# Gate projections of the first layer: float32 products in four column groups in place of split products

## The chip, the core and the metric

The kernel runs on one core of a Trainium2 chip. The metric is the device time of one launch in microseconds (us). Everything below is about the first 30 us of a program that takes about 1465 us.

## The reference

A trunk of two decoder layers over 512 positions of width 1024. Layer 0 mixes tokens by a gated DeltaNet, layer 1 by a Conformer convolution module; each layer then attends to a memory of 256 positions and applies a squared-ReLU MLP. Every sub-layer has an RMS norm before it and a residual after it. The change touches the beginning of layer 0:

```python
h = rms_norm(x, dn_norm)                      # (x * rsqrt(mean(x*x) + eps)) * g
proj = h @ w_in                               # 1024 x (4*1024 + 16)
qkv, z = proj[..., :3072], proj[..., 3072:4096]
b_raw  = proj[..., 4096:4104]                 # one column for each of 8 heads
a_raw  = proj[..., 4104:4112]
qkv = silu(causal_depthwise_conv(qkv, w_conv))
beta = sigmoid(b_raw)
g = -exp(a_log) * softplus(a_raw + dt_bias)
# q, k, v, beta and g then go through the chunked gated delta rule
```

All of it is float32. The sixteen columns of b_raw and a_raw are the "ab" of this document: beta and the decay g of the heads come from them.

## The kernel before, in words

**Products.** Every large matrix product is made of three products in the format fp32r. A tile is split into a high part (a cast to fp32r) and a low part (the tile minus its high part, also fp32r); the kernel sums high·high, high·low and low·high. `mm3` and `proj` issue these three for each of the 8 slices k of 128 input channels (`KT` = 8). Weights arrive as raw float32 tiles of 128 x 1024; ScalarE casts the high part `wh` (L251) and VectorE subtracts to get `wl` (L71). Such a tile serves one output block of 128 channels over all k.

**The input and its norm.** `x` arrives transposed in eight tiles of 128 channels x 512 positions (`load_x`, L103, on the SP queue). `Norm.parts` makes `xh` (ScalarE, L378: x times the norm's gain g, to fp32r) and `xl` (VectorE, L77: x times g minus xh). The factor 1/rms of each position is not in them: it is found later from a second copy of x laid out by position (`xt`, squares on ScalarE at L1541, `stat_tok`), turned into a row on all partitions by TensorE (`spread`, tile `rb`), and multiplied in when a result is taken out of PSUM.

**The first pass.** Head k0 of the key projection is computed in `mm_ab` together with ab. Its weight tile comes in four pieces of 256 columns (`piece`): pieces 0 and 1 are issued on ScalarE's queue, pieces 2 and 3 on SP's between the x tiles. The gain of this norm has a small tile of its own, `gn0` (128 x 8, loaded at L117), and the 16 ab columns of the weight are `wab` (L118, 128 x 128: eight k of 16 columns). On SP's queue the order is x0, gn0, wab, x1, x2, piece 2, x3, x4, piece 3, x5, x6, x7. The order on ScalarE and VectorE is written out by hand (`pin`): a piece's split, then two x tiles' parts, and so on; after the first x tile the split of `wab` into `abp` (16 high and 16 low columns for each k).

For each k TensorE issues three products for head k0 and two for ab: abp's 32 columns (high and low) against xh, and its 16 high columns against xl. They sum into PSUM rows 0 to 31 of one bank: rows 0 to 15 hold the sum of high·high and high·low, rows 16 to 31 low·high.

**What follows.** The list `mains` gives TensorE's order: `mm_ab`, then the heads k1, k2, k3 (each through `halves`: a first part up to k = `cut` and a second part), the four q heads, z, v and so on. Between the parts `run` calls side tasks listed by position. `spread` and `gates_in` (ab times rb, on VectorE) come after the first part of head k2, which has 3 of the 8 k. `gates` comes inside its second part, after k = `CUT_G` = 5: it transposes ab (four TensorE transposes of 32 rows, tile `abT`), adds the two halves on VectorE into `abt`, and computes beta and g from it with small operations. The `ws` machinery (`wnext`, `wsplit`, `wload`) loads and splits weight tiles a few ahead.

Of the kernel before, what the change touches and what calls it, by code (L numbers as in the profile page):

```python
# [8 lines left out]
F32 = mybir.dt.float32  # L9
# [5 lines left out]
P = 128  # L15
# [22 lines left out]
def tile_trunk(ctx, tc, xT, memT, x_d, mem_d, prm_d, adt_d, bdw_d, tap_d, fin_d, w_ab, w_kq, w_v, w_z, w_dno, w_pw1, w_pw2,  # L38
# [56 lines left out]
    prm, gn0 = const([P, NPRM], "prm"), const([P, 8], "gn0")  # L95
# [18 lines left out]
    piece(act, 0)  # L114
    wab = slot(s="wab")[:, 0:P]
    def load_first():
        nc.sync.dma_start(out=gn0, in_=prm_d[:, 0:8])  # L117
        nc.sync.dma_start(out=wab, in_=w_ab)  # L118

    xin = load_x({0: load_first, 2: lambda: piece(nc.sync, 2), 4: lambda: piece(nc.sync, 3)})  # L120
# [185 lines left out]
    def halves(key, hf, xs, reg, name, cut=4, inside=None):  # L306
        st = {}

        def first():
            st["w"] = wnext(key, hf)  # L310
            reg[name] = psum("h")
            proj(st["w"], xs, reg[name], 0, cut)

        return [first, lambda: proj(st["w"], xs, reg[name], cut, 8, inside)]
# [115 lines left out]
    class DeltaNet:  # L430
# [12 lines left out]
        def gates_in(self):  # L443
            self.ab = slot(s="ab")
            tc.keep_in_program_order(tt(dve, self.ab[0:32, :], self.ps.pop("ab")[0:32, :], self.n.rb[0:32, :], ALU.mult))
            dve.tensor_copy(self.tok, self.n.tok)

        def gates(self):
            ab = self.ab
            ps_t = psum("abT")  # L450
            for c in range(4):
                pe.transpose(ps_t[:, c * 32:(c + 1) * 32], ab[0:32, c * P:(c + 1) * P], ident[0:32, 0:32])
            abt, beta, g = self.abt, self.beta, self.g
            abp = ps_t[:, 0:128].rearrange("p (c x) -> p x c", c=4)
            a3 = abt.rearrange("p (x c) -> p x c", c=4)
            dve.tensor_copy(a3, abp[:, 16:32])
            tt(dve, a3, abp[:, 0:16], a3, ALU.add)
# [1047 lines left out]
    abp = slot(F32R, "abp")[:, 0:2 * P]  # L1505
    ab3 = abp.rearrange("p (k x) -> p k x", k=KT)
# [5 lines left out]
    for i in range(4):  # L1512
        s = slice(i * 256, (i + 1) * 256)
        pin(act.copy(hl0[0][:, s], raw0[:, s]))
        pin(tt(dve, hl0[1][:, s], raw0[:, s], hl0[0][:, s].bitcast(F32), ALU.subtract))
        for k in (2 * i, 2 * i + 1):
            n0.parts(k, xin[k], pin)
            if k == 0:
                wab3 = wab.rearrange("p (k x) -> p k x", k=KT)
                pin(act.copy(ab3[:, :, 0:16], wab3))  # L1520
                pin(tt(dve, ab3[:, :, 16:32], wab3, ab3[:, :, 0:16].bitcast(F32), ALU.subtract))
# [30 lines left out]
    def mm_ab():  # L1552
        w = wnext(("k", 0), 0)
        D.ps["ab"], D.ps["k", 0] = psum("ab"), psum("h")
        for k in range(KT):
            (xh, xl), (wh, wl), ps = n0.xs[k], wk(w, k), D.ps["k", 0]
            ab = D.ps["ab"]
            pe.matmul(ps, wh, xh, start=k == 0, stop=False)
# [6 lines left out]
            pe.matmul(ab[0:16, :], abp[:, 32 * k:32 * k + 16], xl, start=False, stop=k == KT - 1)  # L1565
# [151 lines left out]
CUT_G = 5  # L1717
# [70 lines left out]
def _layout(np, i):  # L1788
# [23 lines left out]
    w = i["dn_w_in"][0]  # L1812
    r["w_ab"] = f(w[:, 4096:].reshape(8, 128, 16).transpose(1, 0, 2).reshape(128, 128))
# [32 lines left out]
```

## Time and profile before

| | |
|---|---|
| median of 3 runs | 1465.76 us (1465.67 to 1467.18) |
| profiled execution | 1465.14 us |
| its span, first to last instruction | 1463.4 us |
| TensorE busy | 1452.9 us, 99% |
| VectorE, ScalarE, GpSimd busy | 1065.2, 771.2, 266.8 us |
| first product of head k0 | at 5.36 us |
| second k of head k0 | at 8.06 us |
| first product of head k1 | at 16.35 us |

In the profile PE is TensorE's matmuls and PEld its weight loads, DVE is VectorE, ACT ScalarE, POOL GpSimd, SP the queue that issues most transfers. A row names a line of the kernel, the engine, the operation, the output and inputs with buffer numbers left out, and the shapes. Times count from the start of the span. "idle before, releaser" in a row says how long the engine had been idle and what it had waited for. Matmuls are pipelined: one starts before the duration of the one ahead has run out, so what one costs is read from the distance of their starts.

### The profile page before, as it was taken

The page shows a single profiled execution, that of the slowest core. Times are in us where ns is not written, and L with a number is a line of the kernel's source. Part 1 is how long each engine was busy: PE and PEld are TensorE (multiplying, and loading weights), DVE is VectorE, ACT ScalarE, POOL GpSimd, SP SyncE. Part 2 cuts the span into 40 slices and gives each one's busy share as a digit, 9 for nine tenths or more (in the row PEclk, how much of TensorE's full clock was granted, in tenths as well). Part 3 has the DMA queues.
Part 4 walks back from the last instruction along what each step waited for, and adds up shares of the span by engine and source line. Part 5 has one row for each costly group of instructions (what it writes and reads, how often), then busy time and mean ns, then how long its engine had stood idle before and what let it go on. Part 6 is the DMA issues. An engine that isn't in the chain of part 4 may idle for free.

```text
span 1463.4 us, 19623 instructions
## 1 busy us (share of the span) xinstructions
PE 1452.9 (99%) x7298; PEld 1225.5 (84%) x7298; DVE 1065.2 (73%) x1615; ACT 771.2 (53%) x1326; POOL 266.8 (18%) x289
## 2 busy tenths in 40 slices
PE   9999999999999999999999999999999999999997
PEld 7888889988888888888888889988888888888886
DVE  6879889867646766767679899985555776767677
ACT  7766865655434464435355655564444544434354
POOL 1411310103113000010000486402113010000100
PEclk9999999999999999999999999999999999999999
DMA  8232124442213666584766624533214566575853
GB/s 283 84 115 73 59 87 158 132 143 87 72 44 108 166 165 179 140 199 136 202 159 215 185 82 162 179 129 100 72 51 127 139 169 177 135 210 131 229 144 87
DMA packets 62735, 201.82 MB, mean 138 GB/s; under 512 B 7728, under 2 KB 10032, under 8 KB 62640
## 3 DMA queue, kind: packets, MB, share of 16 engines
q1 hardware_dynamic: 52416, 164.39, 33.4%
q0 software_dynamic: 9792, 35.66, 14.3%
q8 instruction: 57, 0.93, 0.3%
q10 hardware_dynamic: 432, 0.52, 0.1%
q14 instruction: 38, 0.31, 0.1%
HBM read 197.66 MB, written 2.10 MB: 136 GB/s over the span
## 4 chain that ended last, share of the span: by engine, by line
PE 94%; DVE 3%; ACT 2%; DMA 1%; issue 0%; POOL 0%; SPq 0%; POOLq 0%; DVEq 0%
PE up L292 8%; PE up L294 8%; PE up L293 8%; PE dn L1130 6%; PE dn L1128 6%; PE dn L1129 6%; PE pw L294 3%; PE pw L292 3%; PE pw L293 3%; PE h L292 3%; PE h L293 3%; PE h L294 3%; PE xo L293 2%; PE xo L294 2%; PE q L292 2%; PE q L293 2%
## 5 line engine op out<-in xcount | busy, mean ns | idle before, releaser
L251 ACT CAST wh<-raw 128x1024 fp32r<-128x1024 f32 x259 | 271.6, 1051 | 358.7 <-issue 97.0
L71 DVE TENSOR_TENSOR wl<-raw,wh 128x1024 fp32r<-128x1024 f32 (+1 forms) x250 | 304.2, 1219 | 104.3 <-ACT wh L251 98.5
L292 PE MATMUL up<-xh,wh 128*128 128x512 f32 x512 | 199.7, 390 | 0.0
L294 PE MATMUL up<-xh,wl 128*128 128x512 f32 x512 | 199.3, 389 | 0.0
L293 PE MATMUL up<-xl,wh 128*128 128x512 f32 x512 | 199.2, 389 | 0.0
L294 PEld LDWEIGHTS up<-xh,wl 128*128 128x128 f32 x512 | 96.1, 188 | 20.1
L293 PEld LDWEIGHTS up<-xl,wh 128*128 128x128 f32 x512 | 96.2, 188 | 19.8
L292 PEld LDWEIGHTS up<-xh,wh 128*128 128x128 f32 x512 | 96.1, 188 | 19.7
L239 POOL DMA_DIRECT2D t<-w_dn x48 | 42.1, 915 | 354.2 <-DVE wl L71 239.0
L1128 PE MATMUL dn<-wh,ah 128*128 128x512 f32 x256 | 99.8, 390 | 0.0
L1130 PE MATMUL dn<-wl,ah 128*128 128x512 f32 x256 | 99.6, 389 | 0.0
L1129 PE MATMUL dn<-wh,al 128*128 128x512 f32 x256 | 99.6, 389 | 0.0
L77 DVE SCALAR_TENSOR_TENSOR rl<-up,rb 128x512 f32<-128x512 f32 x64 | 44.1, 690 | 58.4 <-PE up L294 58.4
L1358 DVE SCALAR_TENSOR_TENSOR ca<-x,prm,ca 128x512 f32<-128x512 f32 x112 | 82.3, 752 | 3.9 <-ACT ca L1355 1.5
L251 ACT CAST wh<-t 128x1024 fp32r<-128x1024 f32 x44 | 46.4, 1055 | 55.8 <-PE dn L1129 43.7
L71 DVE TENSOR_TENSOR wl<-t,wh 128x1024 fp32r<-128x1024 f32 x44 | 53.7, 1223 | 29.5 <-ACT wh L251 29.3
L292 PE MATMUL h<-xh,wh 128*128 128x512 f32 x184 | 73.7, 400 | 0.0
L71 POOL TENSOR_TENSOR sq<-sq,sq 128x512 f32<-128x512 f32 x28 | 45.4, 1621 | 148.3 <-ACT sq L385 134.2
L294 PE MATMUL h<-xh,wl 128*128 128x512 f32 x184 | 71.9, 391 | 0.0
L293 PE MATMUL h<-xl,wh 128*128 128x512 f32 x184 | 71.7, 390 | 0.0
L71 DVE TENSOR_TENSOR acc<-acc,dn 128x512 f32<-128x512 f32 x100 | 67.3, 682 | 1.2
L71 DVE TENSOR_TENSOR al<-u,ah 128x512 fp32r<-128x512 f32 x64 | 44.1, 688 | 21.4 <-ACT ah L331 21.4
(385 smaller groups left out, 3560.1 us busy)
## 6 DMA issues: line engine op xcount, KB each, us to landing
raw<-w_dn SPq DMA_DIRECT2D x68, 512.0 KB, 3.7
raw<-w_up SPq DMA_DIRECT2D x64, 512.0 KB, 4.3
t<-w_dn POOLq DMA_DIRECT2D x48, 512.0 KB, 6.0
raw<-w_pw SPq DMA_DIRECT2D x24, 512.0 KB, 3.7
raw<-w_dn POOLq DMA_DIRECT2D x20, 512.0 KB, 5.9
raw<-w_k SPq DMA_DIRECT2D x16, 512.0 KB, 3.6
raw<-w_vv SPq DMA_DIRECT2D x16, 512.0 KB, 4.1
t<-w_dn SPq DMA_DIRECT2D x16, 512.0 KB, 3.5
```

The costliest lines, as they stand in the source:

```text
L71: r = e.tensor_tensor(out=o, in0=a, in1=b, op=op)
L77: return dve.scalar_tensor_tensor(out=o, in0=a, scalar=s, in1=b, op0=op0, op1=op1)
L239: nc.gpsimd.dma_start(out=t, in_=a, accum_op=ALU.add)
L251: ins = [act.copy(h, raw)]
L292: pe.matmul(ps, wh, xh, start=first, stop=False)
L293: pe.matmul(ps, wh, xl, start=False, stop=False)
L294: pe.matmul(ps, wl, xh, start=False, stop=last)
L1128: pe.matmul(ps, xh, w[0][:, s], start=opens and k == 0, stop=False, skip_group_check=True)
L1129: pe.matmul(ps, xl, w[0][:, s], start=False, stop=False, skip_group_check=True)
L1130: pe.matmul(ps, xh, w[1][:, s], start=False, stop=k == 3, skip_group_check=True)
L1358: first["tap"] = dve.scalar_tensor_tensor(out=a, in0=src, scalar=w, in1=a, op0=ALU.mult, op1=ALU.add)
```

## The change

The ab products are made from x itself in float32, without xh and xl. `abp` is now `wab` times the gain, a single VectorE product in float32 (16 columns for each k, and 16 zero columns behind the last). Product kk takes 32 columns of it from 16·kk on, of which the first 16 are those of slice kk, and the raw tile `xin[kk]`; it writes PSUM rows 32j to 32j + 31, j = kk mod 4. So the products kk = 0 to 3 go to four different groups of output columns of the array, and kk = 4 to 7 add to the same four. The first four are issued after k = 4 of head k0, the other four after k = 6 (`AB_AT`). The four partial sums are added after the transposes in `gates`, which are now full 128 x 128 transposes, by one VectorE reduction.

The gain `gn0` moves into the first transfer: a new input `first` has in each row 8 gain values and the 256 columns of piece 0, and is issued on ScalarE's queue in place of piece 0. `wab` moves behind x3 on the SP queue, which is then x0, x1, x2, piece 2, x3, wab, x4, piece 3, x5, x6, x7; its product with the gain is pinned behind the parts of x3.

The heads k1 and k2 issue the sixteen products with `wh` first (all k, xh and xl) and then the eight with `wl` (`HIGH_FIRST`); the first part of `halves` is now the sixteen. `CUT_G` is 7, so the transposes of `gates` stand behind the last product of head k2.

```diff
-    prm, gn0 = const([P, NPRM], "prm"), const([P, 8], "gn0")
+    prm, gn0 = const([P, NPRM], "prm"), const([P, 264], "gn0")
...
-    piece(act, 0)
+    act.dma_start(out=gn0, in_=first_d)
     wab = slot(s="wab")[:, 0:P]
-    def load_first():
-        nc.sync.dma_start(out=gn0, in_=prm_d[:, 0:8])
+
+    def load_wab():
         nc.sync.dma_start(out=wab, in_=w_ab)
 
-    xin = load_x({0: load_first, 2: lambda: piece(nc.sync, 2), 4: lambda: piece(nc.sync, 3)})
+    xin = load_x({2: lambda: piece(nc.sync, 2), 3: load_wab, 4: lambda: piece(nc.sync, 3)})
...
         def first():
             st["w"] = wnext(key, hf)
             reg[name] = psum("h")
-            proj(st["w"], xs, reg[name], 0, cut)
-
-        return [first, lambda: proj(st["w"], xs, reg[name], cut, 8, inside)]
+            if name in HIGH_FIRST:
+                for k in range(KT):
+                    for j in range(2):
+                        pe.matmul(reg[name], wk(st["w"], k)[0], xs[k][j], start=(k, j) == (0, 0), stop=False)
+            else:
+                proj(st["w"], xs, reg[name], 0, cut)
+
+        def second():
+            if name in HIGH_FIRST:
+                for k in range(KT):
+                    pe.matmul(reg[name], wk(st["w"], k)[1], xs[k][0], start=False, stop=k == KT - 1)
+                    if inside and k in inside:
+                        inside[k]()
+            else:
+                proj(st["w"], xs, reg[name], cut, 8, inside)
+
+        return [first, second]
...
-            tc.keep_in_program_order(tt(dve, self.ab[0:32, :], self.ps.pop("ab")[0:32, :], self.n.rb[0:32, :], ALU.mult))
+            tc.keep_in_program_order(tt(dve, self.ab, self.ps.pop("ab"), self.n.rb, ALU.mult))
...
-                pe.transpose(ps_t[:, c * 32:(c + 1) * 32], ab[0:32, c * P:(c + 1) * P], ident[0:32, 0:32])
+                pe.transpose(ps_t[:, c * P:(c + 1) * P], ab[:, c * P:(c + 1) * P], ident)
             abt, beta, g = self.abt, self.beta, self.g
-            abp = ps_t[:, 0:128].rearrange("p (c x) -> p x c", c=4)
-            a3 = abt.rearrange("p (x c) -> p x c", c=4)
-            dve.tensor_copy(a3, abp[:, 16:32])
-            tt(dve, a3, abp[:, 0:16], a3, ALU.add)
+            dve.tensor_reduce(out=abt.rearrange("p (x c) -> p x c", c=4),
+                              in_=ps_t.rearrange("p (c y x) -> p x c y", c=4, x=32)[:, 0:16], op=ALU.add, axis=AX.X)
...
-    abp = slot(F32R, "abp")[:, 0:2 * P]
-    ab3 = abp.rearrange("p (k x) -> p k x", k=KT)
+    abp = slot(s="abp")[:, 0:P + 16]
+    pool.memset(abp[:, P:P + 16], 0.0)
...
-        pin(act.copy(hl0[0][:, s], raw0[:, s]))
-        pin(tt(dve, hl0[1][:, s], raw0[:, s], hl0[0][:, s].bitcast(F32), ALU.subtract))
+        src = raw0[:, s] if i else gn0[:, 8:264]
+        pin(act.copy(hl0[0][:, s], src))
+        pin(tt(dve, hl0[1][:, s], src, hl0[0][:, s].bitcast(F32), ALU.subtract))
         for k in (2 * i, 2 * i + 1):
             n0.parts(k, xin[k], pin)
-            if k == 0:
-                wab3 = wab.rearrange("p (k x) -> p k x", k=KT)
-                pin(act.copy(ab3[:, :, 0:16], wab3))
-                pin(tt(dve, ab3[:, :, 16:32], wab3, ab3[:, :, 0:16].bitcast(F32), ALU.subtract))
+            if k == 3:
+                pin(tt(dve, abp[:, 0:P].rearrange("p (k x) -> p k x", k=KT), wab.rearrange("p (k x) -> p k x", k=KT),
+                       over_i(gn0[:, 0:KT], 16), ALU.mult))
...
     def mm_ab():
         w = wnext(("k", 0), 0)
         D.ps["ab"], D.ps["k", 0] = psum("ab"), psum("h")
+        ab = D.ps["ab"]
         for k in range(KT):
             (xh, xl), (wh, wl), ps = n0.xs[k], wk(w, k), D.ps["k", 0]
-            ab = D.ps["ab"]
             pe.matmul(ps, wh, xh, start=k == 0, stop=False)
             pe.matmul(ps, wl, xh, start=False, stop=False)
-            if k:
-                pe.matmul(ab[0:32, :], abp[:, 32 * k:32 * k + 32], xh, start=False, stop=False)
             pe.matmul(ps, wh, xl, start=False, stop=k == KT - 1)
-            if k == 0:
-                pe.matmul(ab[0:32, :], abp[:, 0:32], xh, start=True, stop=False)
-            pe.matmul(ab[0:16, :], abp[:, 32 * k:32 * k + 16], xl, start=False, stop=k == KT - 1)
+            if k in AB_AT:
+                for j in range(4):
+                    kk = 4 * AB_AT[k] + j
+                    pe.matmul(ab[32 * j:32 * j + 32, :], abp[:, 16 * kk:16 * kk + 32], xin[kk], start=kk == j, stop=kk > 3)
...
-CUT_G = 5
+CUT_G = 7
+AB_AT = {4: 0, 6: 1}
+HIGH_FIRST = (("k", 1), ("k", 2))
...
+    r["first"] = f(np.concatenate([r["prm"][:, 0:8], _pack_a(np, w[:, 1024:1280])[0][:, 0:256]], axis=1))
```

More of the change, by code (lines that the diff above doesn't have):

```diff
@@ L37, in tile_trunk @@
 @with_exitstack
-def tile_trunk(ctx, tc, xT, memT, x_d, mem_d, prm_d, adt_d, bdw_d, tap_d, fin_d, w_ab, w_kq, w_v, w_z, w_dno, w_pw1, w_pw2,
+def tile_trunk(ctx, tc, xT, memT, x_d, mem_d, prm_d, adt_d, bdw_d, tap_d, fin_d, first_d, w_ab, w_kq, w_v, w_z, w_dno, w_pw1, w_pw2,
                w_q, w_k, w_vv, w_o, w_up, w_dn, yT):
@@ L1812, in _layout @@
     w = i["dn_w_in"][0]
+    w = i["dn_w_in"][0]
+    r["first"] = f(np.concatenate([r["prm"][:, 0:8], _pack_a(np, w[:, 1024:1280])[0][:, 0:256]], axis=1))
     r["w_ab"] = f(w[:, 4096:].reshape(8, 128, 16).transpose(1, 0, 2).reshape(128, 128))
```

## The prediction

> **What bounds the kernel now.** First the page: busy shares, and the chain that ended last by engine.
>
> ```profile
> PE 1452.9 (99%) x7298; PEld 1225.5 (84%) x7298; DVE 1065.2 (73%) x1615; ACT 771.2 (53%) x1326; POOL 266.8 (18%) x289
> PE 94%; DVE 3%; ACT 2%; DMA 1%; issue 0%; POOL 0%; SPq 0%; POOLq 0%; DVEq 0%
> ```
>
> TensorE is busy almost throughout and the chain lies on it. Busy alone proves little, because matmul ends are modelled, so next the waits of TensorE over the whole span (us in total, times, longest).
>
> ```profile
> PE warm L130 <- POOL ones L127: 1.2, 1, 1.2
> PE h L1558 <- ACT xh L378: 1.0, 1, 1.0
> PE pw L294 <- POOL wl L71: 0.2, 1, 0.2
> PE dn L1130 <- DVE wl L71: 0.2, 1, 0.2
> ```
>
> These are all: 2.2 us at the start, 0.4 us afterwards. So the time falls by what is taken off TensorE, if its inputs keep up. The change works in the first 30 us, so third the chain in order of time (start, length, what), at the start and at some later places.
>
> ```profile
> 0.81 0.38 SPq L103
> 1.25 0.42 SPq L117
> 1.72 0.43 SPq L118
> 2.19 5.08 DMA x<-xT
> 7.29 0.73 ACT xh L378
> 8.06 0.50 PE h L1558
> ...
> 26.52 0.36 PE abT L452 x4
> 26.88 0.43 PE h L292
> ...
> 52.19 0.44 PE kt L586 x4
> 52.63 0.89 PE G L590 x8
> 53.52 0.23 PE h L292
> ```
>
> The path begins on the SP queue: x tile 1 is issued only at 2.19, behind gn (L117) and wab (L118); it lands 5.08 us later, is split, and TensorE starts k = 1 at 8.06. Fourth the timeline, which shows how closely the inputs run beside TensorE.
>
> ```profile
> 6.01 0.28 DVE L71 TENSOR_TENSOR abp<-wab,abp 128x128 fp32r<-128x128 f32 x1
> ...
> 8.04 0.75 DVE L77 SCALAR_TENSOR_TENSOR xl<-x,gn,xh 128x512 fp32r<-128x512 f32 x1 [1.75 <-ACT xh L378]
> ...
> 9.43 0.40 PE L1558 MATMUL h<-xh,wh 128*128 128x512 f32 x1
> ...
> 10.73 1.41 DVE L77 SCALAR_TENSOR_TENSOR xl<-x,gn,xh 128x512 fp32r<-128x512 f32 x2
> ...
> 12.61 0.73 ACT L378 ACTIVATE xh<-x,gn 128x512 fp32r<-128x512 f32 x1 [0.34 <-DMA x<-xT]
> ...
> 13.89 1.05 ACT L251 CAST wh<-raw 128x1024 fp32r<-128x1024 f32 x1 [0.56 <-DMA raw<-w_kq]
> ...
> 14.97 1.22 DVE L71 TENSOR_TENSOR wl<-raw,wh 128x1024 fp32r<-128x1024 f32 x1 [0.85 <-ACT wh L251]
> ...
> 16.35 0.40 PE L292 MATMUL h<-xh,wh 128*128 128x512 f32 x1
> ...
> 19.00 1.05 ACT L251 CAST wh<-raw 128x1024 fp32r<-128x1024 f32 x1
> ...
> 20.09 1.23 DVE L71 TENSOR_TENSOR wl<-raw,wh 128x1024 fp32r<-128x1024 f32 x1 [3.90 <-ACT wh L251]
> ...
> 21.82 0.39 PE L292 MATMUL h<-xh,wh 128*128 128x512 f32 x1
> ...
> 22.97 0.18 DVE L414 RECIPROCAL rstd<-sd 128x4 f32<-128x4 f32 x1 [1.66 <-ACT sd L412]
> ```
>
> A matmul's duration (0.40) is not its price, since the next one starts earlier. From 9.43 (first product of k = 2) to 16.35 (first product of head k1) there are 6 k of 5 products: 6.92 / 30 = 0.231 us each. Head k1 lasts from 16.35 to 21.82, 24 products of 0.228. The last x tile (12.61) and the second weight tile (13.89) waited for DMA, so transfers are not far behind the path.
>
> **What is removed.** Sixteen ab products at 0.231 are 3.7 us of TensorE. One cast on ScalarE and one split on VectorE go; the VectorE product of wab with gn that replaces the split has the same 128x128 shape, 0.28 (row at 6.01), now behind xl of k = 3.
>
> **What is added.** Eight float32 products of 512 columns. The nearest row is G.
>
> ```profile
> L590 PE MATMUL G<-cva 128*128 128x128 f32 x64 | 8.5, 275 | 0.0
> L1565 PE MATMUL ab<-xl,abp 128*16 128x512 f32 x8 | 3.1, 393 | 0.0
> ```
>
> The code asks for 32 G products, the trace counts 64: a float32 product is issued as two halves. In the chain eight halves took 0.89 us, 0.111 each at 128 columns; four times that, 0.445, is my estimate at 512. One after another the eight new products are 16 halves, 7.1 us, twice what is removed: the change pays only if column groups overlap. Before shows no two products at once (the ab product of 16 columns costs as much as any other, but all of them write from partition 0). So a group of four costs between two slots (the four first halves together, then the four second ones, 0.89) and eight (3.56). Going back to the h products costs 0 (after G, 0.23) to 0.20 (after abT, 0.43 instead of 0.23); I take 0.1. I take the low end, G = 0.99, because the four have different weights, different output partitions and no data between them. The Trainium skill (TensorE: Matmul & The Clock Gate, Part 3) reports a speedup of 2.38 for three column tiles; for a group here that is an estimate from that page of 3.56 / 2.38 = 1.5, by which the pass would end at 16.1 instead of the 15.1 found below. No run shown so far decides between them.
>
> **Where the pass ends.** (1) With gn and wab no longer ahead, x tile 1 is issued at 1.25, 0.94 earlier. Its landing gains between 0, if bytes are the limit, and 0.94. The windows (last columns: DMA share, GB/s) say that the DMA engines were busy but moved little while the small packets passed, so I take 0.9.
>
> ```profile
> 4.00:5.00 1.00, 1.00 (x7) 1.00 (x6) 0.29 (x1) 0.72 (x2) 0.00 (x0) 1.00 0.95 172
> ...
> 12.00:13.00 1.00, 1.00 (x6) 0.64 (x5) 1.00 (x3) 0.66 (x2) 0.00 (x0) 1.00 1.03 420
> ```
>
> (2) Then VectorE sets the pace, since TensorE needs only 0.7 us per k there. From the start of xl 1 (8.04) to the end of xl 4 (10.73 + 0.71 = 11.44) it needs 3.40. From 7.14 that gives 10.54, with the new wab product 10.82, and k = 4 is through on TensorE at 11.05. Moving wab behind x tile 3 costs nothing, as long as it lands before 9.5, when VectorE comes to it:
>
> ```profile
> 4.27 0.80 SPq L103 DMA_DIRECT2D x<-xT  x2
> ...
> wab<-w_ab SPq DMA_DIRECT2D x1, 64.0 KB, 3.2
> ```
>
> x tiles 3 and 4 were issued at 4.27 to 5.07 in before, and wab took 3.2 to land (last column), so now it lands near 8; if it came later, everything behind it on VectorE would wait, the remaining xl and so TensorE. (3) From 11.05 on TensorE has two groups and 9 products (k = 5, 6, 7): 11.05 + 9 x 0.231 + 2G = 13.13 + 2G = 15.1. The second group reads x tile 7 directly, landed by 12.61 in before and needed at about 13.5. (4) Against 16.35 that is 1.25 earlier; the break-even is G = 1.61.
>
> **What comes next.** Head k1 needs its weight cast, ready at 13.89 + 1.05 = 14.94: 0.16 of cover. So the gain cannot exceed 1.4, unless that transfer lands earlier too (0.9 at most, by the same queue). Its low part is ready at 16.19; in the old order the third product would ask for it at 15.6 and stall 0.6, in the new order (high products first) after 16 products, at 18.8. For k2 the cast is ready at 20.05, needed at 15.1 + 5.47 = 20.6; the low part at 21.32, needed at 24.2. The spread of rstd (ready 23.15) stands behind those 16 products too, 24.2, and does not wait. So the reordering of k1 and k2 costs nothing and buys 0.6. The evictions that need the spread vector come a little later with it; TensorE does not wait for them in before.
>
> **The gates.** Four 128-column transposes, as kt (0.44), in place of abT (0.36): +0.08 on the path. On VectorE one reduction takes the place of a copy and an add:
>
> ```profile
> 31.21 0.22 DVE L71 TENSOR_TENSOR abt<-abT,abt 128x64 f32<-128x64 f32 x1
> ...
> 40.19 0.37 DVE L503 TENSOR_REDUCE ind<-ident 128x4 f32<-128x128 f32 x1
> ```
>
> A copy and an add of 0.22 against one reduction of 0.37 or somewhat more, with no TensorE wait behind it in before: nothing. With the transposes behind k = 7 of head k2 they come at 26.4, as in before.
>
> **Sum.** -1.25 + 0.08 = -1.17. The profiled execution took 1465.14, 1.74 beyond its span, and lies 0.62 under the median of the runs, 1465.76; on the median that is **1464.6**.
>
> **Rivals.**
>
> *Half-chained groups.* The kernel issues both halves of product 0 before product 1. If a half that waits for its own column group holds up those behind it, only the second half of one overlaps the first half of the next: five slots per group, 2.33, the pass ends at 17.8, +1.5 in all, 1467.3. For it: every float32 row comes as pairs in program order. Against it: nothing measured. The Trainium skill (same page and part) states that matmuls start and end in program order, which is this rival; no row of before has the pattern.
>
> *No overlap, slower.* The column groups do not run at once, so the change does not do what it says: G = 3.56 + 0.1, the pass ends at 20.5, +4.2, 1470.0. For it: the ab products of before filled an eighth or a quarter of the columns and still took a full slot. It decides (over 0.2% slower) from G = 3.03 on.
>
> *A later stretch moves too.* From 142 to 188 us the chain runs on ScalarE and VectorE:
>
> ```profile
> 142.25 0.62 ACT cva L553
> ...
> 187.61 0.58 DVE z L71
> ...
> 100.00:150.00 50.00, 49.91 (x310) 41.78 (x309) 47.75 (x94) 31.84 (x66) 6.13 (x13) 1.00 0.19 64
> ```
>
> VectorE is busy 47.75 of 50 us there. If its or ScalarE's order shifts with the earlier first heads, 2 us may come on top (1462.6 or less) or be lost (up to 1468.5). Against it: the same instructions, released in the same order, all a little earlier.
>
> **Chances.** A measurement of this kernel can tell about 0.2%, 2.9 us, from no change. Forecast, with its bounds (x tile 1 not earlier at all; G up to 1.5): 0.50, all within 0.2%. Half-chained 0.20, within. No overlap 0.14, slower. Later stretch better 0.10, faster; worse 0.06, of it 0.04 slower. That makes 0.10 / 0.72 / 0.18. The range, 1462.2 to 1468.2, leaves out the serial case and the outer parts of the later stretch, 0.2 together.
>
> **What would show it.** Right: ab products of four groups starting within a few ns of each other, groups about 1 us apart from first start to next h product; first product of k = 1 near 7.1; first product of head k1 near 15.1, waiting for nothing or shortly for its cast; abT near 26.4. Wrong: groups of 2.3 or 3.6 us; x tile 1 landing at 7.2 as before; a wait for x tile 7 in front of the second group; new TensorE waits between 100 and 200 us.

## The result and the profile after

After the change the kernel took 1468.0 us, the median of 22 runs (1466.47 to 1468.9), against 1465.72 for the kernel before in 22 runs beside it: ratio 1.0013, 95% interval 1.0007 to 1.0019. It was forecast at 1464.6, that is 1.2 us faster; it is 2.3 us slower. That is within the 0.2% that the prediction takes for no change, but the interval leaves 1 out and lies on the other side. The profiled execution took 1467.88, 1.68 beyond its span of 1466.2.

The first pass did what was forecast. Rows from the timeline of TensorE after the change (start, length):

```profile
6.57 0.40 PE L1570 MATMUL h<-xh,wh 128*128 128x512 f32 x1
...
10.37 1.06 PE L1576 MATMUL ab<-x,abp 128*32 128x512 f32 x8
11.36 0.50 PE L1570 MATMUL h<-xh,wh 128*128 128x512 f32 x1
...
12.95 1.06 PE L1576 MATMUL ab<-x,abp 128*32 128x512 f32 x8
13.95 0.50 PE L1570 MATMUL h<-xh,wh 128*128 128x512 f32 x1
...
14.75 0.40 PE L315 MATMUL h<-xh,wh 128*128 128x512 f32 x1
...
26.47 0.65 PE L466 MATMUL abT<-ident,ab 128*128 128x128 f32 x4 [0.20 <-DVE ab L71]
```

A group of four with its eight halves took 0.99 and 1.00 us from its start to the next h product. Slice k = 1 started at 6.57 (before 8.06), head k1 at 14.75 (before 16.35): 1.6 us won. In the ten other profiled executions below with this first pass head k1 started at 14.82 to 15.25, and in two more with that of before at 16.33 and 16.42, so 1.1 to 1.6 us are won.

The waits of TensorE over the whole span show a new one (us in total, times, longest; the first three):

```profile
PE dt L548 <- DVE L L77: 1.7, 1, 1.7
PE warm L130 <- POOL ones L127: 1.2, 1, 1.2
PE h L294 <- DVE wl L71: 0.3, 1, 0.3
```

`dt` is the product in `decay` (L548) that needs `L`, the last result of the gates. The way there is: `grep`, the end of the gates' small operations on VectorE; `ct`, a product on TensorE that needs it; a copy on ScalarE; then gsum, R and L on VectorE. That place in the timeline of before, which the prediction did not show (rows of this chain, and one of GpSimd):

```profile
40.11 0.16 DVE L492 COPY grep<-g 128x128 f32<-128x128 f32 x1
...
41.92 0.38 PE L515 MATMUL ct<-tri_mid,grep 128*128 128x128 f32 x2
...
42.85 1.30 POOL L71 TENSOR_TENSOR cva<-cva,cvq 128x512 f32<-128x512 f32 x1
42.88 0.61 DVE L71 TENSOR_TENSOR gsum<-ct,gsum 32x128 fp32r<-32x128 f32 x2 [0.48 <-ACT gsum L517]
43.52 1.17 DVE L71 TENSOR_TENSOR R<-gsum,ind 64x512 fp32r<-64x512 f32 x1
...
44.73 0.69 DVE L77 SCALAR_TENSOR_TENSOR L<-gsum,headm 64x512 fp32r<-64x512 f32 x1
44.91 0.30 PE L530 MATMUL gsum<-g,ones 128*128 128x32 f32 x2
...
45.56 1.16 PE L536 MATMUL dt<-R,L 128*128 128x512 f32 x4
...
52.03 0.60 PE L586 MATMUL kt<-ident,cva 128*128 128x128 f32 x4
```

and the same after:

```profile
42.48 0.16 DVE L504 COPY grep<-g 128x128 f32<-128x128 f32 x1
...
42.70 0.49 PE L527 MATMUL ct<-tri_mid,grep 128*128 128x128 f32 x2
...
43.53 0.61 DVE L71 TENSOR_TENSOR gsum<-ct,gsum 32x128 fp32r<-32x128 f32 x2 [0.48 <-ACT gsum L529]
...
44.17 0.72 DVE L71 TENSOR_TENSOR R<-gsum,ind 64x512 fp32r<-64x512 f32 x1
...
44.41 0.30 PE L542 MATMUL gsum<-g,ones 128*128 128x32 f32 x2
...
44.88 1.27 POOL L71 TENSOR_TENSOR cva<-cva,cvq 128x512 f32<-128x512 f32 x1 [0.53 <-ACT cvq L569]
44.92 1.77 DVE L77 SCALAR_TENSOR_TENSOR L<-gsum,headm 64x512 fp32r<-64x512 f32 x1
...
46.84 2.04 PE L548 MATMUL dt<-R,L 128*128 128x512 f32 x4 [1.67 <-DVE L L77]
...
54.87 0.60 PE L598 MATMUL kt<-ident,cva 128*128 128x128 f32 x4
```

Before, L ended at 45.42 and dt began at 45.56. The 0.14 us between them are not slack. After, where TensorE plainly waited, dt also began 0.15 behind the end of L (46.69, 46.84). In the 17 profiled executions of this document dt begins either 0.58 or 0.59 behind the first gsum product, with L done 0.5 us and more before (six executions), or 0.14 to 0.15 behind the end of L (eleven). Before is one of the eleven, with 0.65 behind gsum: TensorE already lost some 0.07 us to L there. The list of waits leaves that out because the modelled end of the product ahead of dt (45.28 + 0.39 = 45.67) lies behind the start of dt. A TensorE that arrives earlier can only wait.

After, TensorE could have begun dt at 44.41 + 0.58 = 44.99, only 0.50 ahead of the 45.49 of before by the same working. At the first product of head k3 it was 1.42 ahead (26.88 against 28.30). About half of what is missing went at 33.81, where a product waited for the low part of a weight tile and started 0.69 behind the one ahead instead of 0.23.

L ended 1.27 later than in before. And from dt to the first kt it took 6.47 us before and 8.03 after, 1.56 more. The windows show what lies there (length; busy PE, PEld, DVE, ACT, POOL; granted clock; DMA share; GB/s):

```profile
46.00:47.00 1.00, 0.16 (x1) 0.19 (x2) 0.97 (x2) 0.09 (x1) 0.14 (x1) 0.90 0.00 0
47.00:50.00 3.00, 3.00 (x8) 2.32 (x9) 3.00 (x5) 2.36 (x5) 0.68 (x3) 0.50 0.03 5
50.00:51.00 1.00, 1.00 (x5) 0.84 (x4) 1.00 (x2) 1.00 (x3) 1.00 (x2) 0.90 0.00 0
```

Behind the idle time TensorE ran at half its clock for 0.2 + 3.0 + 0.2 = 3.4 us (a mean of 0.90 over 1 us is 0.2 us at 0.5). The Trainium skill (TensorE: Matmul & The Clock Gate, Part 1) describes a gate that halves the clock after an idle window of about 3.4 us, and windows that run freely. The 3.4 us at half agree with the length; the idle time ahead of them was only 1.7, so here less than a whole idle window stood ahead of the half clock.

The two together make 1.28 (dt) + 1.56 = 2.84 us at kt, and 2.8 is the difference of the spans. From kt on nothing more is won or lost in sum.

Why L was late is in the chain of after, followed back from L:

```profile
15.83 7.61 DMA raw<-w_kq
23.51 1.06 ACT wh L251
24.59 1.23 DVE wl L71
25.82 0.60 DVE ab L71
...
32.62 1.15 DVE wl L71
33.81 0.50 PE h L294
...
42.74 0.47 PE ct L527 x2
43.23 0.28 ACT gsum L529
...
44.92 1.78 DVE L L77
```

It doesn't pass through the first pass at all. It comes from the transfer of a weight tile, whose low part stands on VectorE in front of ab; it runs over VectorE to another low part, from 33.81 over TensorE to ct, and back to VectorE. Two things changed on the way from before. (1) `grep` came 2.37 later. Of this, ab gives 0.62 (25.73 against 25.11). From ab to grep it took 16.75 instead of 15.00, because VectorE's order changed: one eviction of a head (39.15 to 39.76) and one split of a weight tile (40.05 to 41.19) now stand ahead of grep, which in before came right behind the gates (40.59 and 41.19). TensorE's order changed with it: from ct to gsum there are 6 products of the heads, 12 in before. So before, ct came in its turn 1.65 after grep was ready (40.27, 41.92); after, it came six products later and still waited for grep (42.64, 42.70). gsum began 0.65 later. (2) The GpSimd addition lay beside R in before and beside L after: R took 0.45 less and L 1.08 more. 0.65 - 0.45 + 1.08 = 1.28 is the 1.27 by which L ended later, but for rounding.

### The profile page after: what moved, and what is told of

The parts are those of the page before. It is cut to its first block, busy times and chain, and to the rows that moved or that the text cites. A ratio compares the mean times of both kernels' runs of the same rounds, so it can differ in the third digit from the quotient of the medians.

```text
span 1466.2 us, 19615 instructions
## 1 busy us (share of the span) xinstructions
PE 1454.6 (99%) x7298; PEld 1225.2 (84%) x7298; DVE 1066.2 (73%) x1614; ACT 770.7 (53%) x1325; POOL 266.2 (18%) x290
## 4 chain that ended last, share of the span: by engine, by line
PE 92%; DVE 3%; ACT 2%; DMA 1%; issue 1%; POOL 0%; SPq 0%; ACTq 0%; POOLq 0%; DVEq 0%
PE up L292 8%; PE up L293 8%; PE up L294 8%; PE dn L1142 6%; PE dn L1140 6%; PE dn L1141 6%; PE pw L294 3%; PE pw L292 3%; PE pw L293 3%; PE h L292 2%; PE h L294 2%; PE h L293 2%; PE xo L293 2%; PE xo L292 2%; PE xo L294 2%; PE q L293 2%
## 5 line engine op out<-in xcount | busy, mean ns | idle before, releaser
L292 PE MATMUL h<-xh,wh 128*128 128x512 f32 x168 | 67.7, 403 | 0.0
L294 PE MATMUL h<-xh,wl 128*128 128x512 f32 x168 | 65.9, 393 | 0.3 <-DVE wl L71 0.3
L293 PE MATMUL h<-xl,wh 128*128 128x512 f32 x168 | 65.7, 391 | 0.0
```

Source lines behind the costliest of these rows:

```text
L292: pe.matmul(ps, wh, xh, start=first, stop=False)
L293: pe.matmul(ps, wh, xl, start=False, stop=False)
L294: pe.matmul(ps, wl, xh, start=False, stop=last)
```

## Experiments

Theory from here on: the 1.3 to 1.6 us are won in the first pass; VectorE's L, which nothing in the change makes earlier, takes them back, and the idle time at dt costs TensorE's clock on top. Rivals: the loss comes from the new order of heads k1 and k2, or from other results that come late next. What the engines' orders of work have to do with it shows only across the runs, and stands behind the last of them. All kernels are edits of after unless before is named; ratios are against before on the same chip.

### Filling the wait

Seven products into a scratch bank, placed ahead of the first dt, keep TensorE busy while it waits.

```diff
                 ps = psum("dt")
+                if h == 0:
+                    for _ in range(7):
+                        tc.keep_in_program_order(pe.matmul(ps, self.xs[0][0][:, 0:P], self.xs[0][0], start=True, stop=True))
```

> The changed kernel, with seven extra products of 128x512 (xh against xh, into the bank of the first dt product, which overwrites them) put on TensorE right before the four dt products, where it waited 1.67 us. Theory (the loss is a wait of TensorE for L, and the half clock that follows the idle time): 7 x 0.228 = 1.6 us of work lie inside the wait, so dt still starts near 46.8, but the clock stays at 1.00 from 46 to 50 us; kt of the first head moves from 54.9 to about 53.4, and the time from 1468.0 to about 1466.5 (ratio to before near 1.0005). Rival (the half clock has another cause than the idle time, or the later start of dt alone makes the loss): the clock is 0.50 again or kt stays near 54.9, and the time stays at 1468 or grows by up to 1.6.

1466.61 us, 1.4 below after (ratio 1.0006, 0.9997 to 1.0015). L ended at 47.00 in this execution, dt began at 47.15, and the first kt at 53.60 instead of 54.87, at full clock. The number is the theory's. How much of it is the clock is not shown: the wait does not always lose the clock, and in a profile of after that kept it (below) kt came at 53.72, only 0.12 later than here.

### Dt one unit later

```diff
-    S.at(T_DEC, 2, D.decay, [0, 1, 2, 3])
+    S.at(T_DEC + 1, 2, D.decay, [0, 1, 2, 3])
```

> The changed kernel, with the decay step (the gsum and dt products) placed one unit later in TensorE's order, so that twelve products of the next q head (2.7 us) stand in front of it. VectorE's order up to L is the same. Theory (wait for L and half clock): TensorE finds L ready, no wait and no half clock between 44 and 51 us; the 1.3 us won in the first pass stay, kt of the first head near 51 to 52 instead of 54.9, and the time is about 1464.4, ratio to before 0.999. Rival (VectorE is the bound from 24 us to well behind 50 us, and whatever TensorE wins is given back at its next results): a new wait behind kt, and the time near that of before or above, 1465.7 to 1467.

1469.31 us (ratio 1.0026, 1.0016 to 1.0036), the slowest of all. The wait for L is gone, and three others stand in its place:

```profile
PE h L292 <- ACT egd L545: 1.8, 1, 1.8
...
PE mg L701 <- DVE x L692: 1.1, 1, 1.1
PE z L339 <- DVE bt L71: 0.8, 1, 0.8
```

The theory's 1464.4 failed. The first kt came at 51.29, earlier than in before, so dt itself was no longer in the way. But `egd`, the exponential of gsum on ScalarE, moved with dt. It began only at 54.24, behind a `cva` for which ScalarE had waited 1.67 us for VectorE (52.30) and a table load of 1.28 (52.95), and a product of the heads waited for it. The longest new wait is thus made by the edit together with VectorE's lateness; the run does not part the two.

### All taps of the first key heads behind L

```diff
-TAPK = {2: 12, 3: 12}
+TAPK = {0: 12, 1: 12, 2: 12, 3: 12}
```

> The changed kernel, with the convolution taps of the key heads 0 and 1 (six VectorE operations, 4.05 us, which stood between the ab transposes' reduction and the gates) queued behind L, as those of heads 2 and 3 already are. Theory (VectorE, full from 24.6 us on, makes L late): L is done 2 to 4 us earlier, dt follows gsum without a wait, no half clock, the time is about 1464.4, ratio near 0.999. Rival (the order of the splits inside the gates' chain makes L late, not the amount of work): two splits still stand inside the chain, L is late by the same and the time stays near 1468. Second rival: the taps moved behind L make kt late instead, TensorE waits there, 1466 to 1468.

1465.79 us (ratio 1.0, 0.9992 to 1.0009). L ended at 45.09, dt did not wait, but the taps themselves were late then: kt waited 1.8 us for `cva`. The second rival's wait came, though the time lies just below its 1466: six VectorE operations are too many to move.

### The old order of k1, k2 and the gates

```diff
-CUT_G = 7
-HIGH_FIRST = (("k", 1), ("k", 2))
+CUT_G = 5
+HIGH_FIRST = ()
```

> The changed kernel, with the old order of the heads k1 and k2 and the transposes of ab after k = 5 again (no high products first): only the ab products in column groups and the loads are left of the change. VectorE's order is then close to that of before, with the splits outside the gates' chain. Theory A (any earlier TensorE runs into L): stalls of 0.5 to 1 us for the low part of k1's weight and for rstd at 16 to 23 us take most of the gain already there, dt waits less, no half clock: 1465 to 1466. Theory B (the head order alone makes the loss, by the splits that it lets into the gates' chain): L 1 to 2 us earlier than in the changed kernel, 1464 to 1465. If the ab products or the loads are the cause, the time stays at 1468.

1466.23 us (ratio 1.0, 0.9991 to 1.0009), 1.8 below after. The waits show where the lead went:

```profile
PE abT L466 <- DVE ab L71: 0.8, 1, 0.8
PE rb L376 <- DVE rstd L428: 0.8, 1, 0.8
```

It is spent on two waits before 28 us. L took 0.69 and ended at 46.35; dt began at 46.50, 0.83 behind gsum, so it too was held by L, by some 0.25 us. So with the old order the loss against before is gone, but the gain does not come: the time is nearest to theory A. The engines' orders are those of before again: 12 products between ct and gsum, 14.48 us from ab to grep, and the GpSimd addition at 43.66, ahead of L. The new order of the heads therefore has its part in the loss, through what it moves on VectorE and TensorE between 27 and 45 us.

### The same work, later

Six more products (`pad`) at the end of the first pass, 1.4 us of TensorE.

```diff
-    mains.extend([mm_ab, lambda: None, lambda: None, lambda: None])
+    mains.extend([lambda: (mm_ab(), pad()), lambda: None, lambda: None, lambda: None])
```

> The changed kernel, with six extra products of 128x512 (into a bank that nothing reads) at the end of the first pass, 1.4 us more work for TensorE, so that head k1 starts near 16.1 instead of 14.75. Theory (VectorE, full from rb on, sets when L is ready; an early TensorE only waits longer for it): dt starts near 46.8 as in the changed kernel, the wait in front of it shrinks to about 0.3, the clock stays at 1.00, kt of the first head near 53.4 instead of 54.9: 1466.5, faster than the changed kernel by 1.5 with 1.4 us more work. Rival (TensorE's work counts everywhere): 1469.4.

1467.99 us (ratio 1.0018, 1.0009 to 1.0027), about the same as after, for 1.4 us more work: neither expectation. Head k1 started at 16.30 as in before, but the spread came later too (the copy of rb at 26.01 against 24.47), so that ab and L moved with it (L to 47.58) and dt, at 47.73, waited 1.67 again. Against a profile of after with the full clock (below), dt is 0.49 later, not 1.4. So L is not fixed in time either: the spread stands in TensorE's order behind head k2's high products, and a later pass can make L later. The clock stayed at 1.00 there.

### The spread earlier

The spread is put in front of the last four high products of k2, and the cast of the fourth weight tile behind the copy of rb.

```diff
-                for k in range(KT):
-                    for j in range(2):
-                        pe.matmul(reg[name], wk(st["w"], k)[0], xs[k][j], start=(k, j) == (0, 0), stop=False)
+                high(0, 6 if name == ("k", 2) else KT)
...
-        with tc.issue_after(ws["rb"].ins) if u == 4 else nullcontext():
+        with tc.issue_after(ws["rb"].ins) if u in (3, 4) else nullcontext():
...
```

> The changed kernel, with rb earlier: head k2's first part is 12 high products instead of 16, so that the spread of rstd stands where rstd is ready (22.9 instead of 23.8), and ScalarE copies rb ahead of the cast of the fourth weight tile, which waited for its transfer until 23.5. VectorE then starts on ab and the evictions near 24.0 instead of 25.7, and has no idle 1.56 us in front. Theory (rb and VectorE's stretch behind it are the path between 23 and 56 us): L 0.7 to 1.5 earlier, dt near 45.3 to 46, wait below 0.7, no half clock, kt near 52, time 1464.7 to 1465.5, ratio near 0.9995. Rival (the path there is something else, such as the weight tiles' transfers): the fourth tile's cast and split come late for head k3, TensorE waits near 27, and the time is 1466 to 1468.

1466.96 us (ratio 1.001, 1.0001 to 1.0018); the forecast of 1464.7 to 1465.5 failed. In this execution rstd was ready only at 24.19, so the earlier spread waited 0.8 us for it; ab came at 25.55, L stretched to 1.78 again, and dt waited 1.2.

### Key head 0's taps alone behind L

```diff
-TAPK = {2: 12, 3: 12}
+TAPK = {0: 12, 2: 12, 3: 12}
```

> The changed kernel, with the taps of key head 0 alone (three VectorE operations, 2.0 us) queued behind L; those of head 1, whose kt comes first, stay. Theory: L 1.5 to 2 us earlier, dt near 45.2 behind gsum without a wait, no half clock; kt of head 1 near 51.5; the kt of head 0 may wait. Time 1464.8 to 1465.8. Rival: as with both heads' taps moved, a wait at kt gives everything back, 1465.8 or more.

1464.16 us (ratio 0.9989, 0.998 to 0.9997), faster than both kernels. Three VectorE operations, some 2 us, leave the stretch before L. The line does more than that: the engines' orders around ct are those of before again (12 products between ct and gsum; the eviction and the split behind grep), so that from ab to grep it takes 12.45 us instead of 16.75, and the GpSimd addition (40.92) lies ahead of L. Its rows:

```profile
42.21 0.68 DVE L71 TENSOR_TENSOR R<-gsum,ind 64x512 fp32r<-64x512 f32 x1
42.92 0.69 DVE L77 SCALAR_TENSOR_TENSOR L<-gsum,headm 64x512 fp32r<-64x512 f32 x1
...
43.57 0.30 PE L542 MATMUL gsum<-g,ones 128*128 128x32 f32 x2
...
44.15 1.17 PE L548 MATMUL dt<-R,L 128*128 128x512 f32 x4
...
50.63 0.60 PE L598 MATMUL kt<-ident,cva 128*128 128x128 f32 x4
```

dt starts 1.41 earlier than in before and does not wait; kt starts 1.40 earlier, and the span, 1461.8, is 1.6 shorter. What the first pass won is kept to the end once L is not in the way.

### Two products in each column group

Products 0 and 1 write the same 32 rows, 2 and 3 the next, and so on, so that a batch of four uses two column groups.

```diff
-                    pe.matmul(ab[32 * j:32 * j + 32, :], abp[:, 16 * kk:16 * kk + 32], xin[kk], start=kk == j, stop=kk > 3)
+                    r = 32 * (kk // 2)
+                    pe.matmul(ab[r:r + 32, :], abp[:, 16 * kk:16 * kk + 32], xin[kk], start=kk % 2 == 0, stop=kk % 2 == 1)
```

> The changed kernel, with the ab products 0 and 1 both in the first column group, 2 and 3 in the second, 4 and 5 in the third, 6 and 7 in the fourth: two groups at once instead of four in each batch. The batch took 0.99 us to the next h product in the changed kernel. If each column group has its own order (a half waits only for its own group), a batch is 4 slots of 0.43 and takes about 1.8; if a half that waits holds up those behind it, 7 slots, 3.0; if groups did not overlap at all, 3.5. The whole time: TensorE later by 1.6 (4 slots) is hidden before dt, 1466 to 1467; by 4 it is not, 1468 to 1470.

One run, 1468.12 us. The first batch (the second starts at 13.92 and takes as long):

```profile
10.48 1.92 PE L1577 MATMUL ab<-x,abp 128*32 128x512 f32 x8
12.33 0.50 PE L1570 MATMUL h<-xh,wh 128*128 128x512 f32 x1
```

1.85 us a batch is four slots of some 0.44 and the 0.1 of going back. In program order the four halves of one group come first, then the four of the other. If a waiting half held up those behind it, only the last half of the one group would overlap the first of the other: seven slots, 3.1 us. So each column group goes by its own order here, and the half-chained rival is refuted. The records show it directly: told apart by the transfer that each waits for, product 2, the first of the second group, starts at 10.497, 0.013 behind product 0, and product 1, ahead of it in the program, only at 10.94. Head k1 started at 16.57, 1.8 later than in after, and dt, which waited 1.7 us for L here too, at 47.98, only 1.1 later; the clock stayed at 1.00, which made up for that. The batch came as expected for groups with their own order; the time of this one run lies above the 1466 to 1467 expected with it.

### Before with the tap order

> The kernel before, with one line changed: the convolution taps of key head 0 are put behind L, as in the run that kept the lead (after with the same line took 1464.2). Theory (the new first pass wins 1.3 to 1.6 us, and the order of VectorE's work before L only decides whether that is kept): in before dt had no wait, so the line has nothing to give; 1465.7, within 0.6, dt at 45.6 as in before. Rival (the tap order is itself what gained, and the new first pass counts for little): 1464.2 or less, with dt or kt earlier than in before by 1 us and more.

1464.89 us (ratio 0.9996, 0.9987 to 1.0005). dt at 45.55 and kt at 52.03, as in before, although L ended 0.67 ahead of dt here, which is the theory's; the time is 0.9 below before, which is not, though the interval holds 1.

### The tap order with the old loads

After with key head 0's taps behind L, and gn0 and wab back in the order of before.

```diff
-    act.dma_start(out=gn0, in_=first_d)
+    act.dma_start(out=gn0[:, 8:264], in_=first_d[:, 8:264])
...
+        nc.sync.dma_start(out=gn0[:, 0:8], in_=prm_d[:, 0:8])
...
-    xin = load_x({2: lambda: piece(nc.sync, 2), 3: load_wab, 4: lambda: piece(nc.sync, 3)})
+    xin = load_x({0: load_wab, 2: lambda: piece(nc.sync, 2), 4: lambda: piece(nc.sync, 3)})
```

> After with the taps of key head 0 behind L, and with the loads put back in the order of before (the first norm's vector again by small packets, wab behind x tile 0, so x tile 1 is issued 0.9 us later and lands later). Theory (the prediction's first step: the earlier x tile 1 is worth about as much at the end of the pass, VectorE setting the pace): first product of k = 1 near 8.0 instead of 6.6, head k1 near 15.6 to 16.0 instead of 14.75, and 1465.0 to 1465.5 instead of 1464.2. Rival (the column groups alone won it, the weight tile of head k1 or another transfer hides the rest): head k1 at 14.8 and 1464.2, within 0.4.

1465.06 us (ratio 0.9996, 0.9987 to 1.0005), 0.9 above the kernel with the new loads, which was measured on another chip. Head k1 began late, and dt with it:

```profile
15.98 0.40 PE L316 MATMUL h<-xh,wh 128*128 128x512 f32 x1
...
45.03 1.17 PE L549 MATMUL dt<-R,L 128*128 128x512 f32 x4
```

Head k1 and dt are both 0.88 later than with the new loads (15.10 and 44.15), and dt is 0.53 earlier than in before. By this pair of executions some 0.9 of the lead at dt come from the loads and 0.5 from the products. The split is not sure: in a second execution of the kernel with the new loads (the last experiment) dt started at 45.48. Slice k = 1 started at 6.55 here, against the 8.0 expected, although x tile 1 was again issued at 2.19: it was not the one held up, and the wait for xh was one slice later (0.34 at 8.19). The price came out the same.

### Both moves

After with key head 0's taps behind L and the earlier spread.

> After with the taps of key head 0 behind L, and the spread of rstd moved up in front of the last four high products of head k2 (with the cast of the fourth weight tile behind its copy). Theory (with the taps behind L no result is late on TensorE any more, so an earlier spread has nothing left to give): 1464.2, within 0.6. Rival (the spread, which starts VectorE's full stretch at 24.5, still sets what follows): 1463.5 or less. Third: the spread waits for rstd on TensorE as it did for 0.8 us in the run with the spread alone, and nothing takes that back: 1465.0.

1463.72 us (ratio 0.9986, 0.9977 to 0.9995), the lowest median of all; 1464.16 without the earlier spread lies inside its runs (1463.4 to 1465.17). The spread adds nothing that these runs can tell. The profiled execution, at 1465.17 the slowest of them, waited 0.6 for L.

### After once more

> After, unchanged, a second time. Theory (two losses: dt waits for L in every execution; TensorE's clock is at half rate behind that wait in some executions only): the wait of about 1.7 us in front of dt again, the granted clock from 47 to 50 us either 0.5 or 1.0, and 1468.0, within 0.5. Rival (the half clock follows from the wait each time): 0.5 again in the same place.

1467.45 us (ratio 1.0012, 1.0003 to 1.0021). dt waited 1.68 again, and the clock stayed up:

```profile
47.00:50.00 3.00, 2.75 (x12) 2.31 (x13) 2.97 (x6) 2.25 (x5) 0.58 (x1) 1.00 0.02 5
```

kt at 53.72 is then 1.69 later than in before. TensorE had also waited 0.9 us for a weight's low part ahead of ct (0.3 in the first profile of after), a further wait of 0.6 follows kt (G for kt), and the execution took 1467.29, 2.15 above the profiled one of before. So the loss is there without the half clock. Of the five profiled executions in which dt waited 1.2 us or more (this one, after, the padding, the pairs, the spread) only after lost its clock. They do not sort by length: 1.67 lost it; 1.68, 1.67, 1.66 and 1.23 kept it. How often it happens over all runs, and what decides it, is open.

### The GpSimd addition taken away

One GpSimd addition of a tap of query head 0 is left out, and with it that tap.

```diff
-                    tt(pool, a, a, b, ALU.add)
+                    if ti:
+                        tt(pool, a, a, b, ALU.add)
```

> After without the one GpSimd addition of a convolution tap for query head 0 (that tap is left out of that head), which ran beside VectorE's L in after (GpSimd 44.88 to 46.15, L 1.77 instead of 0.69). Theory (that addition stretches L by 1.08, and dt waits for L): L 0.69 again, dt's wait 0.6 instead of 1.7, and 1.1 less than after: 1466.9; 0.5 to 1.5 less again if the shorter wait leaves TensorE's clock alone more often. Rival (L is slow by itself there, or another result is late next): L 1.7 or a new wait, 1468.0.

1466.77 us (ratio 1.0006, 0.9996 to 1.0015), 1.2 below after; 1.1 was expected.

```profile
PE dt L548 <- DVE L L77: 0.6, 1, 0.6
...
46.14 0.69 DVE L77 SCALAR_TENSOR_TENSOR L<-gsum,headm 64x512 fp32r<-64x512 f32 x1
```

L is back at 0.69, and the wait shrinks by 1.08. So this addition, which came to lie beside L by the new order, is what stretches L. dt itself did not start earlier in this execution (46.98), since gsum came 1.23 later than in after, behind a wait of 1.0 for a weight's low part. That the 1.2 us are the stretch alone is therefore likely, not shown; against the second median of after (1467.45) it is 0.7. The Trainium skill (SBUF — State Buffer, SBUF: two separate sides) says that GpSimd and a VectorE operation with two SBUF inputs share a port pair, and that the one that starts later blocks for the whole of the other's instruction. The trace is near that: L started 0.04 behind the addition, which ended at 46.15, and L ended at 46.69, 0.54 later. The same holds where this addition met L or R: in seven profiled executions L, and in three (before, and both of before with the tap order) R, ended 0.53 to 0.56 behind the end of the addition, however far they had overlapped.

### The tap order, with and without the change, side by side

> After with the taps of key head 0 behind L, beside before with the same line on the same chip. Theory (the new first pass wins 1.3 to 1.4 us at dt and that stays): 1.0 to 1.5 below before with the line. Rival (the line itself is most of the gain): less than 0.5 below it.

> Before with the taps of key head 0 behind L. Theory (dt had no wait in before, nothing to win): equal to before, within 0.3; the 0.9 less of the first such run is spread. Rival (the line is worth 0.9 by itself): 1464.9 again.

After with the line 1463.8 us (ratio 0.999, 0.9981 to 0.9998), before with the line 1464.73 (0.9995, 0.9986 to 1.0004). With the first such run of each, 22 runs on either side, the medians are 1463.95 and 1464.84. With the tap order the change wins 0.9 us; the theory's 1.0 to 1.5 was a little high. Its profile shows why it is not always 1.4: abT waited 0.9 us for ab there, and dt started at 45.48, 0.08 ahead of before. The line alone came out 0.9 and 0.7 below before; each interval holds 1, but two independent runs point the same way. In the profile of before some 0.07 us are lost at dt; that executions in which ab is late lose more there would fit, but it is argued, not shown, as none of before with a longer hold at dt was profiled. In the second profile of before with the line, abT waited 1.1 us for ab and dt still did not wait for L. The old loads with the tap order (1465.06) are no faster than before with it (1464.84), so what the column groups win without the new loads does not show in the times.

One thing runs through all the profiles, though no run was built for it. In seven profiles (after twice, the filling, the padding, the pairs, dt one unit later, and the earlier spread alone) grep starts at 42.3 to 43.6, ct comes late in TensorE's order, and the GpSimd addition lies beside L, which takes 1.77 to 1.81. In the nine profiles with 12 products between ct and gsum (before, the old order, and all with key heads' taps newly behind L), grep starts at 37.9 to 40.9 and L takes 0.69. The old order of the heads and the tap order each bring that back, and with each the 2.3 us of loss are gone. So an edit can move a step that it doesn't touch to another place in an engine's order.

## Why the prediction was wrong

**Right.** The price of a group was 0.99 and 1.00 us, forecast 0.99: the low end between 0.89 and 3.56 was the true one. The Trainium skill's 2.38 for three column tiles (TensorE: Matmul & The Clock Gate, Part 3), by which a group would take 1.5, does not hold for these four. The pass ended at 14.75, forecast 15.1 (14.82 to 15.25 in ten other executions). The gates cost nothing up to abT (26.47, forecast 26.4). No overlap and half-chained groups, with 0.34 between them, are refuted by the groups and by the pairs.

**Right in number only.** The term for x tile 1 was to come from its earlier issue. k = 1 started at 6.57, forecast 7.1; but with gn and wab ahead again it started at 6.55 too. The 0.9 that the old loads cost arose one slice later, so the place was wrong, and that the size agrees is at least partly luck.

**Wrong.** The step that failed is "What comes next", together with "The gates". The first followed the results that TensorE needs only to abT at 26.4. The second put the gates behind abT at nothing, "with no TensorE wait behind it in before". So the -1.25 went straight into the sum. A list of waits says who waits, not by how little the others don't, and it leaves out a wait that the modelled end of the product ahead covers. The rows of L (44.73, 0.69), gsum (44.91) and dt (45.56) stood in the trace: at dt, L had no slack at all. With TensorE 1.25 earlier there and L where it was, the same working would have given no gain. Had L moved up with TensorE's ct, VectorE's idle time ahead of gsum (0.48 at 42.88) bounds the gain at about 0.5, an estimate from that row. The term of the sum should have been -0.5 to 0 in place of -1.25.

The loss of 2.3 us could not be read from these rows. In the profile L moved 1.27 us later: gsum by 0.65, because VectorE's and TensorE's orders ahead of it changed, and L by a stretch of 1.08 beside GpSimd's addition, less 0.45 at R. And in that execution TensorE's clock was halved for 3.4 us, 1.56 more. "The same instructions, released in the same order", which the prediction holds against its rival "a later stretch moves too", is what did not hold. That rival did see VectorE as a danger, with "better" and "worse" at 0.10 and 0.06, and up to 1468.5. That 1468.0 lies inside the stated range, which ends at 1468.2, is luck: the rival looked at 142 to 188 us, where the chain lies on VectorE in before. The place was 45 us, where the chain lay on TensorE and VectorE was as full: 17.33 of the 18 us from 24 to 42.

```profile
24.00:30.00 6.00, 6.00 (x32) 4.76 (x30) 5.92 (x10) 4.58 (x6) 0.00 (x0) 1.00 0.94 372
30.00:36.00 6.00, 6.00 (x28) 4.98 (x27) 6.00 (x10) 4.10 (x5) 0.20 (x2) 1.00 0.28 88
36.00:42.00 6.00, 6.00 (x28) 4.96 (x27) 5.41 (x24) 2.28 (x7) 1.25 (x2) 1.00 0.54 187
```

**Open.** How often the clock is lost at dt; and why ab comes between 24.7 and 27.2 from one kernel and execution to the next (in after the landing of a weight tile stood ahead of it), which moves L by as much.

## What to carry to other kernels

Before a gain on the bounding engine is added to the sum, follow that engine to the next results of each other engine that is nearly full, and read how long each had been ready. A result that came 0.14 us ahead of its reader here had no slack: the same 0.14 to 0.15 stood there when the reader waited. The smallest true slack is the gain, until that engine's work is moved too. Afterwards, compare the engines' orders, not only their times. Here one line, which moves three VectorE operations behind the result in demand and brings the old order around it back, turned +2.3 us into -1.6 against before, somewhat more than half of it by the change. A wait on TensorE may also cost more than its length, because its clock may go down behind it; one of five executions showed that.

## What was not expected of the hardware

- Float32 products in different column groups overlap fully: eight halves in two slots, 0.99 us with the way back, where one after another they would take 8 x 0.445 = 3.56; and each group keeps only its own order (pairs: 1.85 us).
- Behind 1.7 us without work TensorE ran 3.4 us at half its clock in one of five executions; in four, behind 1.2 to 1.7 us, it did not.
- A VectorE operation of 0.69 us took 1.77 beside a GpSimd addition, and 0.69 again without it; it ended 0.54 behind the addition's end.
